# Seven block products of sums in place of eight, in three chunks of each feed-forward of a float32 trunk

## The chip, the cores and the metric

The kernel runs on one core of a Trainium2 chip. The metric is the device time of one launch in microseconds (us), the median of three runs.

## The reference

Four layers, each a half-step feed-forward, an attention (three kinds by turns) and a second half-step feed-forward, on 256 tokens of width 1024, all in float32. The eight feed-forwards are what the change touches:

```python
def rms_norm(x, g, eps=NORM_EPS):
    xf = x.astype(jnp.float32)
    y = xf * lax.rsqrt(jnp.mean(xf * xf, axis=-1, keepdims=True) + eps)
    return (y * g.astype(jnp.float32)).astype(x.dtype)
def swiglu(x, w_in, w_out):
    gate, up = jnp.split(x @ w_in, 2, axis=-1)
    return (jax.nn.silu(gate) * up) @ w_out
```

A half step is h + 0.5 * rms_norm(swiglu(rms_norm(h, g_pre), w_in, w_out), g_post), with w_in 1024 x 5632 and w_out 2816 x 1024.

## The kernel before, in words

The 256 tokens are two tiles t = 0, 1 of 128. For each product the transposed tokens are the weights of TensorE (stationary) and the weight matrix streams past them. Both are split exactly into hi (rounded to float32r) and lo (the rest), and a product is hi x hi + lo x hi + hi x lo: three matmuls for each 128 rows of K. `hilo` (L146) is the split: ScalarE rounds hi (L147), VectorE subtracts to get lo (L148).

`ffn` (L257) cuts the inner width 2816 into five full chunks of 512 (j = 0 to 4) and one of 256 (j = 5). A **unit** (`unit`, L114) is 1 MB of weights, 512 rows by 512 columns of w_in or 256 rows by 1024 of w_out: one DMA on SyncE's queue into a `raw` buffer, then two hi and two lo instructions of 128x1024 each. There are 3 raw buffers, 4 hi/lo pairs for w_in (`wt`) and 3 for w_out (`wo`); a unit waits for its buffer to come free, so the pools decide how far ahead of TensorE the splits run.

In a chunk j from 1 to 4, TensorE runs gate and up for both token tiles (`gate_up`, `product`: four products of 24 matmuls of 512 columns, L144), the four transposes of the result of tile 0 (`turn`, L298), the out product of chunk j-1 for tile 0 (24 matmuls, L236 to L238), the transposes of tile 1 and the out product of tile 1. The transposes are split again into gh (ScalarE) and gl (VectorE, L148). Between these, ScalarE takes silu of the gate (L286) and VectorE multiplies it with up (g, L289).

After the last chunk the feed-forward ends with `finish`: y's mean square, then on VectorE the next sub-layer's input xg (L212, L214), then the update of h (L217, L219), for tile 0 while TensorE still multiplies for tile 1. xg is transposed (tpx, L172) and split into xh and xl, with which the next sub-layer begins.

Each engine works through its own instructions in a fixed order, which is laid down when the program is built; an instruction that waits holds up all that stand behind it on its engine.

## Time and profile before

| | |
|---|---|
| median of 3 runs | 2032.63 us (2032.4 to 2033.66) |
| span of the profiled execution | 2031.3 us |
| TensorE (PE) busy | 2005.6 us, 99% |
| VectorE (DVE) busy | 1260.2 us, 62% |
| ScalarE (ACT) busy | 1033.0 us, 51% |
| TensorE's granted clock | 9 in every slice (90% of full speed or more) |

The span lies 1.33 us below the median. Busy shares are means over the program; within one chunk of a feed-forward they differ, so stretches are read on their own. Matmuls overlap: the time that one adds is the distance from its start to the next one's start, its pitch, not its duration. The same holds for rows of VectorE with a count: first start to last end, of overlapped instructions.

### The profile page before, as it was taken

How to read it: one execution, taken by the hardware profiler on the slowest of the kernel's cores; microseconds unless marked ns; L12 is line 12 of the kernel's file. 1: busy time of each engine (PE TensorE's matmuls, PEld its weight loads, DVE VectorE, ACT ScalarE, POOL GpSimd, SP SyncE). 2: the span in 40 equal slices, each digit the busy share in tenths (PEclk: the TensorE clock that was granted, in tenths of full speed). 3: DMA queues.
4: the chain of work that ended last, by engine and by line, in shares of the span. 5: the costliest groups of instructions: out<-in, count | busy, mean ns of one | idle time of the engine just before them, and what ended most of it. 6: DMA issues, size and time to landing. Idle time of an engine off the chain costs nothing.

```text
span 2031.3 us, 26240 instructions
## 1 busy us (share of the span) xinstructions
PE 2005.6 (99%) x10096; PEld 1659.2 (82%) x10096; DVE 1260.2 (62%) x2051; ACT 1033.0 (51%) x1713; POOL 118.6 (6%) x239
## 2 busy tenths in 40 slices
PE   8999999999999999999999999999999999999998
PEld 6888878888888878888888888678888888878887
DVE  6645678545745666844665568875547545678542
ACT  6443566443543466543454456764445443676441
POOL 0000210000000120000000032000000000210000
PEclk9999999999999999999999999999999999999999
DMA  8654436654656353755376556147554654437550
GB/s 301 224 182 175 163 109 212 224 189 163 210 185 207 125 186 100 254 191 202 125 248 204 203 121 185 44 133 250 197 200 171 209 190 155 157 104 240 205 186 22
DMA packets 168654, 363.19 MB, mean 179 GB/s; under 512 B 7760, under 2 KB 36688, under 8 KB 168528
## 3 DMA queue, kind: packets, MB, share of 16 engines
q1 hardware_dynamic: 168528, 361.51, 52.4%
q8 instruction: 79, 1.29, 0.3%
q14 instruction: 47, 0.39, 0.1%
HBM read 360.43 MB, written 1.05 MB: 178 GB/s over the span
## 4 chain that ended last, share of the span: by engine, by line
PE 94%; DVE 3%; ACT 2%; POOL 1%; issue 0%; DMA 0%; SPq 0%; DVEq 0%; POOLq 0%; ACTq 0%
PE ps L144 47%; PE y L238 9%; PE y L236 9%; PE y L237 9%; PE pw L434 4%; PE pw L435 3%; PE pw L436 3%; PE tpg L298 2%; PE sc L508 1%; DVE lo L148 1%; PE tpx L172 1%; PE tpp L533 1%; PE o L579 1%; PE tpf L465 1%; ACT e L519 0%; ACT hi L147 0%
## 5 line engine op out<-in xcount | busy, mean ns | idle before, releaser
L148 DVE TENSOR_TENSOR lo<-raw,hi 128x1024 fp32r<-128x1024 f32 (+1 forms) x670 | 782.9, 1209 | 481.9 <-ACT hi L147 481.0
L147 ACT CAST hi<-raw 128x1024 fp32r<-128x1024 f32 (+1 forms) x670 | 659.9, 1036 | 412.0 <-PE ps L144 128.6
L144 PE MATMUL ps<-hi,xh 128*128 128x512 f32 (+1 forms) x1536 | 573.6, 373 | 1.2 <-ACT xh L147 1.2
L144 PE MATMUL ps<-hi,xl 128*128 128x512 f32 (+1 forms) x1536 | 572.1, 372 | 0.0
L144 PE MATMUL ps<-lo,xh 128*128 128x512 f32 (+1 forms) x1536 | 571.4, 372 | 0.0
L144 PEld LDWEIGHTS ps<-hi,xh 128*128 128x128 f32 x1536 | 290.0, 189 | 50.8 <-ACT xh L147 1.6
L144 PEld LDWEIGHTS ps<-hi,xl 128*128 128x128 f32 x1536 | 289.8, 189 | 50.9 <-DVE xl L148 0.8
L144 PEld LDWEIGHTS ps<-lo,xh 128*128 128x128 f32 x1536 | 290.1, 189 | 49.9 <-DVE lo L148 0.2
L236 PE MATMUL y<-hi,gh 128*128 128x512 f32 x704 | 281.6, 400 | 0.0
L237 PE MATMUL y<-lo,gh 128*128 128x512 f32 x704 | 274.7, 390 | 0.0
L238 PE MATMUL y<-hi,gl 128*128 128x512 f32 x704 | 274.1, 391 | 0.0
L434 PE MATMUL pw<-hi,xh 128*128 128x512 f32 (+2 forms) x432 | 164.5, 381 | 0.2 <-ACT nat L445 0.2
L286 ACT ACTIVATE sl<-ps,st 128x512 f32<-128x512 f32 (+1 forms) x96 | 62.6, 652 | 196.2 <-issue 149.3
L238 PEld LDWEIGHTS y<-hi,gl 128*128 128x128 f32 x704 | 132.1, 188 | 29.2 <-DVE gl L148 1.3
L435 PE MATMUL pw<-lo,xh 128*128 128x512 f32 (+2 forms) x432 | 155.8, 361 | 0.0
L436 PE MATMUL pw<-hi,xl 128*128 128x512 f32 (+2 forms) x432 | 155.5, 360 | 0.0
L236 PEld LDWEIGHTS y<-hi,gh 128*128 128x128 f32 x704 | 132.3, 188 | 26.0 <-ACT gh L147 1.7
L237 PEld LDWEIGHTS y<-lo,gh 128*128 128x128 f32 x704 | 132.5, 188 | 24.9
L111 POOL TENSOR_TENSOR st<-st,negh 128x1 f32<-128x1 f32 (+1 forms) x56 | 36.8, 658 | 1689.6 <-DVE st L195 1626.3
L147 ACT CAST gh<-tpg 128x512 fp32r<-128x512 f32 (+1 forms) x96 | 51.8, 548 | 150.1 <-PE tpg L298 149.9
L289 DVE SCALAR_TENSOR_TENSOR g<-ps,st,sl 128x512 f32<-128x512 f32 (+1 forms) x96 | 67.5, 704 | 92.9 <-PE ps L144 92.8
L148 DVE TENSOR_TENSOR gl<-tpg,gh 128x512 fp32r<-128x512 f32 (+1 forms) x96 | 61.0, 643 | 62.6 <-ACT gh L147 62.4
(165 smaller groups left out, 1778.2 us busy)
## 6 DMA issues: line engine op xcount, KB each, us to landing
raw<-in_ffn_w_in SPq DMA_DIRECT2D x172, 1024.0 KB, 5.3
raw<-in_ffn_w_out SPq DMA_DIRECT2D x88, 1024.0 KB, 4.9
raw<-in_diff_w_in SPq DMA_DIRECT2D x24, 1024.0 KB, 5.1
raw<-in_moba_w_in SPq DMA_DIRECT2D x12, 1024.0 KB, 5.2
raw<-in_nsa_w_in SPq DMA_DIRECT2D x9, 1024.0 KB, 6.1
raw<-in_diff_w_out SPq DMA_DIRECT2D x8, 1024.0 KB, 4.9
gpre<-in_norm_g SPq DMA_DIRECT2D x12, 512.0 KB, 3.8
gpost<-in_norm_g SPq DMA_DIRECT2D x12, 512.0 KB, 3.8
```

The lines of the kernel that those rows point to most:

```text
L144: nc.tensor.matmul(out, l, r, start=first and i == 0, stop=last and i == len(steps) - 1)
L147: self.nc.scalar.copy(hi, src)
L148: self.nc.vector.tensor_tensor(lo, src, hi.bitcast(F32), op=ALU.subtract)
L236: nc.tensor.matmul(y[b], x[0][:, kt, :], hi[:, k, s], start=f, stop=False)
L237: nc.tensor.matmul(y[b], x[0][:, kt, :], lo[:, k, s], start=False, stop=False)
L238: nc.tensor.matmul(y[b], x[1][:, kt, :], hi[:, k, s], start=False, stop=l)
L286: nc.scalar.activation(sl[t][:, :w], ps[:, :w], AF.Silu, scale=X[t][1])
L289: nc.vector.scalar_tensor_tensor(g[:, :w], ps[:, :w], X[t][1], sl[t][:, :w], op0=ALU.mult, op1=ALU.mult)
L298: nc.tensor.transpose(tp[:, k, :], g[:, k * P:(k + 1) * P], self.ident)
L434: nc.tensor.matmul(out, x[0][:, kt, :], hi[:, k, :], start=first and i == 0, stop=False)
L435: nc.tensor.matmul(out, x[0][:, kt, :], lo[:, k, :], start=False, stop=False)
L436: nc.tensor.matmul(out, x[1][:, kt, :], hi[:, k, :], start=False, stop=last and i == len(todo) - 1)
```

## The change

In chunks 1, 2 and 3 of each feed-forward (`WINO`), gate and up of both token tiles are taken as one 2 x 2 block product (Strassen's in Winograd's form). The tokens are halved by tile and by K (a00 and a01 are tile 0's two halves of K, a10 and a11 tile 1's), the weights by K and by gate/up (b00, b10 gate; b01, b11 up). Seven half-K products of 12 matmuls take the place of eight, of these blocks and sums of them, and their PSUM results are added up.

- `sums` makes the token sums, once for each feed-forward, from the transposed tokens that `xturn` now also copies aside (`keep`): four VectorE instructions of 128x512, and their own hi and lo (sh, sl).
- `plan_wino` makes four weight sums per chunk on VectorE, 128x2048 each: t1 = b00 + b01, t2 = t1 + b11, t3 = b01 + b11, t4 = t2 + b10.
- `wino` runs the seven products into three PSUM banks (pa, pb, pc), copies one to SBUF (p1), and makes gate and up from them with five more VectorE additions of 128x512 (u2, v, g1, g0, sl1) beside the two multiplications that were there.
- Seven units (b00, t2, t3, b10, t1, b11, t4) instead of four are split for each of these chunks, and every split is one hi and one lo instruction of 128x2048 instead of two of 128x1024.
- All weights of a feed-forward, w_out's too, go through one ring: 7 raw buffers (t1 and t2 take two of them) and 4 hi/lo pairs, filled in one list's order (`loads`, `preps`, `fill`). The four PSUM banks of products and transposes are one pool.
- At a feed-forward's end the transposes of chunk 5's tile 1, `turn(last, 1)`, move behind `end(0, ...)` and tile 1's out product of chunk 4.

The built program holds 9758 matmul instructions of TensorE before and 9470 after: 288 fewer, 12 in each of 24 chunks.

```diff
@@ constants and pools @@
+RAWS = 7
+UNITS = 4
+WINO = (1, 2, 3)
...
-        self.wt = pool("wt", 4)
+        self.wt = pool("wt", UNITS)
...
-        self.mm = pool("mm", 2, space=PSUM)
-        self.tp = pool("tp", 2, space=PSUM)
+        self.mm = self.tp = pool("mm", 4, space=PSUM)
...
@@ xturn @@
+        if keep:
+            self.nc.scalar.copy(x.rearrange("p (k n) -> p k n", n=P)[:, 4 * b:4 * b + 4, :], tp)
...
@@ sums @@
+    def sums(self, X, pool, name):
+        v = self.nc.vector
+        half = [[X[t][2][:, b * 512:b * 512 + 512] for b in range(2)] for t in range(NT)]
+        (a00, a01), (a10, a11) = half
+        v.tensor_tensor(a11, a11, a10, op=ALU.subtract)
+        v.tensor_tensor(a10, a00, a10, op=ALU.subtract)
+        v.scalar_tensor_tensor(a00, a11, -1.0, a00, op0=ALU.mult, op1=ALU.subtract)
+        v.scalar_tensor_tensor(a01, a01, -1.0, a00, op0=ALU.mult, op1=ALU.subtract)
+        out = []
+        for t in range(NT):
+            sh = pool.tile([P, KD, P], F32R, tag="sh", name=f"sh{name}_{t}")
+            sl = pool.tile([P, KD, P], F32R, tag="sl_", name=f"sl_{name}_{t}")
+            src = X[t][2].rearrange("p (k n) -> p k n", n=P)
+            self.hilo(src, sh, sl)
+            out.append((sh, sl))
+        return out
...
@@ ffn @@
-                self.tc.tile_pool(name=f"wo{l}{f}", bufs=3, reuse_waits="tile") as wo:
...
+            def split(n, of, done=False):
+                live["unit"] += 1
+                self.n += 1
+                nk, w, m = shape.get(of, (4, 512, 4))
+                hi = self.wt.tile([P, nk, w], F32R, tag="hi", name=f"hi{self.n}")
+                lo = self.wt.tile([P, nk, w], F32R, tag="lo", name=f"lo{self.n}")
+                v = R[of][:, :nk * w].rearrange("p (k n) -> p k n", n=w)
+                for k in range(0, nk, m):
+                    self.hilo(v[:, k:k + m], hi[:, k:k + m], lo[:, k:k + m])
+                if done:
+                    free(of)
+                U[n] = hi, lo, nk, w
...
+                for n, src in (("b00", quarter(0, 0)), ("b01", quarter(0, 1)), ("t1", None), ("t2", None),
+                               ("b11", quarter(1, 1)), ("b10", quarter(1, 0))):
+                    loads.append(lambda n=n, src=src: raw(name(n), src))
...
+                def t12():
+                    add("t1", "b00", "b01")
+                    add("t2", "t1", "b11")
+                    split(name("t2"), name("t2"))
+                def t3():
+                    add("b01", "b01", "b11")
+                    split(name("t3"), name("b01"), True)
+                def t4():
+                    add("t2", "t2", "b10")
+                    free(name("b10"))
+                    split(name("t4"), name("t2"), True)
...
+                preps.append((name("b00"), lambda: split(name("b00"), name("b00")), 4))
+                preps.append((name("t2"), lambda: (t12(), free(name("b00"))), 6))
+                preps.append((ko[0], lambda: split(ko[0], ko[0], True), 5))
+                preps.append((name("t3"), t3, 0))
+                preps.append((name("b10"), lambda: split(name("b10"), name("b10")), 2))
+                preps.append((name("t1"), lambda: split(name("t1"), name("t1"), True), 0))
+                preps.append((ko[1], lambda: split(ko[1], ko[1], True), 1))
+                preps.append((name("b11"), lambda: split(name("b11"), name("b11"), True), 0))
+                preps.append((name("t4"), t4, 0))
+            def fill():
+                while loads and live["raw"] < RAWS:
+                    loads.pop(0)()
+                while preps and live["unit"] < UNITS:
+                    preps.pop(0)[1]()
+                    while loads and live["raw"] < RAWS:
+                        loads.pop(0)()
...
+            def wino(j, nr):
+                def times(ps, x, at, n, first, stop, shut=True):
+                    self.product(ps, x, [(at, unit((j, n)))], first, stop, more=True)
+                    close((j, n))
+                def o(t, k):
+                    out(j - 1, t, (k,))
+                    if t == 1:
+                        close((j - 1, "o", k))
+                    fill()
+                two = lambda name: pool.tile([P, 512], F32, tag=name, name=f"{name}{l}{f}_{j}", bufs=1)
+                add = lambda d, x, z: nc.vector.tensor_tensor(d, x, z, op=ALU.add)
+                (s24, s31), A, B, C = SUMS, bank("pa"), None, None
+                p1, u2, v = two("p1"), two("u2"), two("v")
+                times(A, X[0][0], 0, "b00", True, True)
+                nc.scalar.copy(p1, A)
+                fill()
+                turn(j - 1, 0)
+                B = bank("pb")
+                times(B, s24, 0, "t2", True, True)
+                add(u2, B, p1)
+                fill()
+                o(0, 0)
+                C = bank("pc")
+                times(C, s31, 0, "t3", True, True)
+                fill()
+                turn(j - 1, 1)
+                times(A, X[0][0], 4, "b10", False, True)
+                sl0 = gate(0, A, 512, j)
+                fill()
+                o(1, 0)
+                times(B, s31, 4, "t1", False, True)
+                add(v, B, p1)
+                g1 = pool.tile([P, 512], F32, tag="g", name=f"g{l}{f}_{j}_1")
+                add(g1, C, v)
+                fill()
+                o(0, 2)
+                times(B, s24, 4, "b11", False, True)
+                g0 = pool.tile([P, 512], F32, tag="g", name=f"g{l}{f}_{j}_0")
+                add(g0, B, p1)
+                up(0, g0, 512, sl0, j, nr[0], g0)
+                fill()
+                times(C, X[1][0], 4, "t4", False, True)
+                sl1 = pool.tile([P, 512], F32, tag="sl", name=f"sl{l}{f}_{j}_1")
+                add(sl1, C, u2)
+                nc.scalar.activation(sl1, sl1, AF.Silu, scale=X[1][1])
+                up(1, g1, 512, sl1, j, nr[1], g1)
...
-            gate_up(last)
-            u = out_units(last - 1)
-            out(last - 1, 0, u)
-            turn(last, 0)
-            turn(last, 1)
-            ahead()
-            u2 = out_units(last)
-            out(last, 0, u2)
-            turn_x = end(0, y[0])
-            out(last - 1, 1, u)
-            turn_x()
-            out(last, 1, u2)
-            self.later_x = end(1, y[1])
+            plain(last, zig, [lambda: turn(last - 1, 0), lambda: turn(last - 1, 1)])
+            out(last - 1, 0, (0, 2))
+            turn(last, 0)
+            ahead()
+            out(last, 0, (0,))
+            turn_x = end(0, y[0])
+            out(last - 1, 1, (0, 2))
+            for k in (0, 2):
+                close((last - 1, "o", k))
+            turn(last, 1)
+            turn_x()
+            out(last, 1, (0,))
+            self.later_x = end(1, y[1])
```

What VectorE's order becomes between the second and the third of the full chunks 1 to 3, shown in layer 1's first feed-forward. Before, from the end of chunk 2's splits to chunk 3's g (g_j_t and gl_j_t carry chunk and tile):

```order
L148 TENSOR_TENSOR lo_4906<-raw_4903,hi_4905 128x1024
L148 TENSOR_TENSOR gl_2_0_4803<-tpg_2_0_4797,gh_2_0_4802 128x512
L148 TENSOR_TENSOR lo_4906<-raw_4903,hi_4905 128x1024
L148 TENSOR_TENSOR lo_5031<-raw_5028,hi_5030 128x1024 x2
L148 TENSOR_TENSOR gl_2_1_4852<-tpg_2_1_4846,gh_2_1_4851 128x512
L148 TENSOR_TENSOR lo_5039<-raw_5036,hi_5038 128x1024 x2
L148 TENSOR_TENSOR lo_5104<-raw_5101,hi_5103 128x1024 x2
L148 TENSOR_TENSOR lo_5112<-raw_5109,hi_5111 128x1024 x2
L289 SCALAR_TENSOR_TENSOR g_3_0_4990<-ps_3_10_4965,st_4161,sl_3_0_4936 128x512
L148 TENSOR_TENSOR lo_5120<-raw_5117,hi_5119 128x1024 x2
L289 SCALAR_TENSOR_TENSOR g_3_1_5017<-ps_3_11_4992,st_4247,sl_3_1_4963 128x512
```

After, the same stretch:

```order
L364 TENSOR_TENSOR raw_4724<-raw_4655,raw_4674 128x2048
L473 TENSOR_TENSOR g_2_0_4848<-pb_4706,p_2_4677 128x512
L364 TENSOR_TENSOR raw_4754<-raw_4724,raw_4801 128x2048
L419 SCALAR_TENSOR_TENSOR g_2_0_4848<-g_2_0_4848,st_4444,sl_2_0_4776 128x512
L473 TENSOR_TENSOR sl_2_1_4871<-pc_4737,u_2_4678 128x512
L364 TENSOR_TENSOR raw_4674<-raw_4674,raw_4801 128x2048
L152 TENSOR_TENSOR lo_4854<-raw_4754,hi_4853 128x2048
L419 SCALAR_TENSOR_TENSOR g_2_1_4818<-g_2_1_4818,st_4446,sl_2_1_4871 128x512
L152 TENSOR_TENSOR lo_4876<-raw_4782,hi_4875 128x2048
L152 TENSOR_TENSOR lo_4895<-raw_4674,hi_4894 128x2048
L152 TENSOR_TENSOR lo_4918<-raw_4803,hi_4917 128x2048
L152 TENSOR_TENSOR gl_2_0_4927<-tpg_2_0_4921,gh_2_0_4926 128x512
```

Between a chunk's g and the next one's stand the additions of 128x2048 (L364: t1, t2, t3 of chunk 3), and the splits of t2, of a w_out unit, t3 and b10, all behind one another; the multiplications and additions for g stand between them.

VectorE at the end of layer 0's second feed-forward (gl_5_t is the split of chunk 5's transposes). Before:

```order
L148 TENSOR_TENSOR gl_5_0_4088<-tpg_5_0_4084,gh_5_0_4087 128x256
L148 TENSOR_TENSOR gl_5_1_4095<-tpg_5_1_4091,gh_5_1_4094 128x256
L193 TENSOR_SCALAR st_4130<-st_4128 128x1
L212 TENSOR_TENSOR yx_4139<-y_0_0_3193,gpre_4098 128x512
L195 SCALAR_TENSOR_TENSOR st_4135<-st_4133,st_4130 128x1
L212 TENSOR_TENSOR yx_4139<-y_0_1_3194,gpre_4098 128x512
L214 SCALAR_TENSOR_TENSOR xg_4100<-yx_4139,st_4137,xg_4100 128x512 x2
L217 TENSOR_TENSOR yg_4146<-y_0_0_3193,gpost_2925 128x512
L217 TENSOR_TENSOR yg_4146<-y_0_1_3194,gpost_2925 128x512
L219 SCALAR_TENSOR_TENSOR h_85<-yg_4146,st_4137,h_85 128x512 x2
```

After:

```order
L201 SCALAR_TENSOR_TENSOR st_4118<-st_4116,st_4113 128x1
L218 TENSOR_TENSOR yx_4122<-y_0_1_3103,gpre_4089 128x512
L220 SCALAR_TENSOR_TENSOR xg_4091<-yx_4122,st_4120,xg_4091 128x512 x2
L223 TENSOR_TENSOR yg_4129<-y_0_0_3102,gpost_2927 128x512
L223 TENSOR_TENSOR yg_4129<-y_0_1_3103,gpost_2927 128x512
L225 SCALAR_TENSOR_TENSOR h_82<-yg_4129,st_4120,h_82 128x512 x2
L152 TENSOR_TENSOR lo_4265<-raw_4248,hi_4264 128x2048
L199 TENSOR_SCALAR st_4137<-st_4135 128x1
L152 TENSOR_TENSOR gl_5_1_4174<-tpg_5_1_4170,gh_5_1_4173 128x256
L152 TENSOR_TENSOR xl_4124<-tpx_4177,xh_4123 128x512
```

gl_5_1, which stood right behind gl_5_0 and ahead of `finish`, now stands behind tile 0's yx, xg, yg and h and behind a lo of 128x2048 of the next sub-layer.

## Rows read from the trace of the kernel before

**Rows 1.** Page: busy time by engine; share of the last chain by engine.
```profile
PE 2005.6 (99%) x10096; PEld 1659.2 (82%) x10096; DVE 1260.2 (62%) x2051; ACT 1033.0 (51%) x1713; POOL 118.6 (6%) x239
...
PE 94%; DVE 3%; ACT 2%; POOL 1%; issue 0%; DMA 0%; SPq 0%; DVEq 0%; POOLq 0%; ACTq 0%
```
**Rows 2.** Chain of waits, in one full chunk: start, us, what.
```profile
1059.96 15.42 PE ps L144 x68
1075.38 0.44 PE tpg L298 x4
```
**Rows 3.** Windows, one chunk: PE, PEld, DVE, ACT, POOL; clock, DMA share, GB/s.
```profile
1062.90:1096.50 33.60, 33.60 (x154) 27.78 (x153) 16.68 (x16) 14.09 (x18) 0.00 (x0) 1.00 0.56 188
```
**Rows 4.** Timeline of VectorE, the same chunk: start, us, what, [idle before].
```profile
1015.39 4.63 DVE L148 TENSOR_TENSOR lo<-raw,hi 128x1024 fp32r<-128x1024 f32 x4 [0.99 <-ACT hi L147]
...
1062.94 2.36 DVE L148 TENSOR_TENSOR lo<-raw,hi 128x1024 fp32r<-128x1024 f32 x2 [8.58 <-ACT hi L147]
...
1076.10 0.75 DVE L289 SCALAR_TENSOR_TENSOR g<-ps,st,sl 128x512 f32<-128x512 f32 x1
1076.76 1.22 DVE L148 TENSOR_TENSOR lo<-raw,hi 128x1024 fp32r<-128x1024 f32 x1
1077.89 0.68 DVE L148 TENSOR_TENSOR gl<-tpg,gh 128x512 fp32r<-128x512 f32 x1
1078.49 3.49 DVE L148 TENSOR_TENSOR lo<-raw,hi 128x1024 fp32r<-128x1024 f32 x3
...
1096.57 2.36 DVE L148 TENSOR_TENSOR lo<-raw,hi 128x1024 fp32r<-128x1024 f32 x2 [8.57 <-ACT hi L147]
```
**Rows 5.** VectorE by line and shape: busy us, mean ns, idle before.
```profile
L148 DVE TENSOR_TENSOR lo<-raw,hi 128x1024 fp32r<-128x1024 f32 x650 | 769.6, 1225 | 477.9 <-ACT hi L147 477.0
...
L1046 DVE TENSOR_TENSOR gpre<-gpre,gpost 128x1024 f32<-128x1024 f32 x11 | 13.7, 1248 | 1.6 <-DMA gpost<-in_norm_g 1.4
...
L148 DVE TENSOR_TENSOR lo<-raw,hi 128x512 fp32r<-128x512 f32 x16 | 10.1, 681 | 3.8 <-ACT hi L147 3.8
```
**Rows 6.** ScalarE by line and shape.
```profile
L147 ACT CAST hi<-raw 128x1024 fp32r<-128x1024 f32 x650 | 648.3, 1048 | 409.8 <-PE ps L144 128.6 <-issue 96.2 <-PE y L238 66.9
...
L147 ACT CAST hi<-raw 128x512 fp32r<-128x512 f32 x16 | 9.0, 618 | 2.2 <-DMA raw<-in_ffn_w_in 2.1
```
**Rows 7.** Timelines of VectorE, ScalarE and TensorE at a feed-forward's end.
```profile
190.03 0.76 DVE L148 TENSOR_TENSOR gl<-tpg,gh 128x256 fp32r<-128x256 f32 x2 [2.61 <-ACT gh L147]
...
194.68 1.42 DVE L214 SCALAR_TENSOR_TENSOR xg<-yx,st,xg 128x512 f32<-128x512 f32 x2
...
197.34 1.41 DVE L219 SCALAR_TENSOR_TENSOR h<-yg,st,h 128x512 f32<-128x512 f32 x2
...
193.15 0.60 ACT L190 ACTIVATE junk<-y 128x512 f32<-128x512 f32 x1 [0.73 <-PE y L238]
...
197.88 1.03 PE L172 MATMUL tpx<-ident,xg 128*128 128x128 f32 x8
```
**Rows 8.** Windows, the program's start; columns as in rows 3.
```profile
11.00:15.30 4.30, 4.16 (x9) 2.98 (x10) 4.30 (x8) 4.27 (x10) 0.55 (x1) 1.00 1.05 385
```
**Rows 9.** DMA issues: line, queue, count, KB each, median us to landing.
```profile
raw<-in_ffn_w_in SPq DMA_DIRECT2D x172, 1024.0 KB, 5.3
```
**Rows 10.** Timeline of TensorE after two of its waits.
```profile
11.14 0.79 PE L144 MATMUL ps<-hi,xh 128*128 128x512 f32 x1 [1.18 <-ACT xh L147]
...
15.31 0.47 PE L144 MATMUL ps<-hi,xh 128*128 128x512 f32 x1
...
1229.56 0.65 PE L465 MATMUL tpf<-ident,nat 128*128 128x128 f32 x4 [1.38 <-POOL nat L458]
...
1230.29 0.28 PE L436 MATMUL pw<-hi,xl 128*128 128x256 f32 x1
1230.41 0.28 PE L434 MATMUL pw<-hi,xh 128*128 128x256 f32 x1
```

More of the change, by code (lines that the diff above doesn't have):

```diff
@@ L131, in split_unit, with product @@
         return hi, lo, nk, w
-    def product(self, out, x, units, first=True, last=True, cols=None):
+    def product(self, out, x, units, first=True, last=True, cols=None, more=False):
         nc = self.nc
@@ L143, in product @@
         for i, (l, r) in enumerate(steps):
-            nc.tensor.matmul(out, l, r, start=first and i == 0, stop=last and i == len(steps) - 1)
+            nc.tensor.matmul(out, l, r, start=first and i == 0, stop=last and i == len(steps) - 1,
+                             skip_group_check=more)
     def hilo(self, src, hi, lo):
@@ L197, in mean_square, with finish @@
         return v
-    def finish(self, t, y, gpost, half, x=None, gg=None):
+    def finish(self, t, y, gpost, half, x=None, gg=None, keep=False):
         nc = self.nc
@@ L221, in finish @@
             rest = self.rms(t)
[L222 removed]
+            return (X, rest, x), lambda: [self.xturn(x, b, X, keep) for b in range(2)]
         return None, lambda: None
@@ L328, in ffn, with plain @@
-            ahead()
-            u2 = out_units(last)
-            out(last, 0, u2)
-            turn_x = end(0, y[0])
-            out(last - 1, 1, u)
+                n = chunks[j][1] // P
+                self.out_product(t, y[t], G[j, t], [(k, unit((j, "o", k))) for k in ks],
+                                 j == 0 and 0 in ks, j == last and n - 2 in ks)
+            def plain(j, order, between=()):
+                w = chunks[j][1]
+                hs = (0, 1) if w == 512 else (0,)
+                between = list(between)
+                sl = {}
+                for i, (which, t) in enumerate(order):
+                    ns = [(j, "gu"[which], h) for h in hs]
+                    ps = bank("ps")
+                    self.product(ps[:, :w], X[t][0], [(4 * h, unit(n)) for h, n in zip(hs, ns)])
+                    self.turn_x()
+                    if which == 0:
+                        sl[t] = gate(t, ps, w, j)
+                    else:
+                        up(t, ps, w, sl[t], j, X[t][1])
+                    if (which, 1 - t) in order[:i]:
+                        for n in ns:
+                            close(n)
+                    fill()
+                    if between:
+                        between.pop(0)()
@@ new lines, in ffn @@
+            plan_plain(0)
+            for j in range(1, last):
+                if j in WINO:
+                    plan_wino(j)
+                else:
+                    plan_plain(j)
+                    plan_out(j - 1)
+            plan_plain(last)
+            plan_out(last - 1)
+            plan_out(last)
+            plain(0, [(0, 0), (1, 0), (0, 1), (1, 1)])
+            if WINO:
+                SUMS = self.sums(X, pool, f"{l}{f}")
+                nr = []
+                for t in range(NT):
+                    r = self.stat()
+                    nc.vector.tensor_scalar(r, X[t][1], -1.0, None, op0=ALU.mult)
+                    nr.append(r)
@@ L1048, in end @@
             def end(t, y):
-                after[t], turn_x = self.finish(t, y, gpost, kind == "ffn", xs[t], gg)
+                keep = not last and phases[i + 1][1] == "ffn"
+                after[t], turn_x = self.finish(t, y, gpost, kind == "ffn", xs[t], gg, keep)
                 if last:
```

152 lines of the change are left out of this document (100 added, 52 removed).

## Prediction, made before the changed kernel was run

> **What bounds the kernel now.** First the page: TensorE is busy 99% of the span, VectorE 62%, ScalarE 51%, and the chain that ends last is TensorE's for 94% [rows 1]. Next, what TensorE does inside a chunk: in the chain of waits 68 matmuls of 512 columns take 15.42 us, so each adds 0.2268 us, and a group of four transposes adds 0.44 us [rows 2]. A full chunk has 96 matmuls for gate and up, 48 for the out product and two groups of transposes: 144 x 0.2268 + 0.88 = 33.54 us. The same place in the next chunk comes 1096.57 - 1062.94 = 33.63 us later [rows 4]. So TensorE does nothing but multiply there, at granted clock 1.00, the 2.4 GHz level [rows 3].
>
> The page's 62% for VectorE is a mean. In a chunk it works 16.68 us of 33.60, ScalarE 14.09 [rows 3]. This half-empty VectorE is what the change spends, and the window, not the page, is where it is priced.
>
> **What TensorE saves.** 288 matmuls x 0.2268 = 65.3 us, if every one was on the end-setting path and nothing else becomes late. A changed chunk is 132 x 0.2268 + 0.88 = 30.8 us of TensorE.
>
> In rows 2 the pitch is 226.8 ns. The Trainium skill ("TensorE: Matmul & The Clock Gate", section "Back-to-back issue gap") gives about 131 ns for sustained matmuls of 512 columns; by that the saving would be an estimated 37.7 us and the time 27.6 us above what each case below says. The trace does not agree, and its number is used.
>
> **What VectorE is given.** Its operation of 128x2048 has no row. The 128x1024 subtraction lasts 1.225 us, the 128x512 one 0.681 [rows 5], so a further element costs 544/512 = 1.0625 ns. Back to back, four of 1024 end after 4.63 us [rows 4], so one adds (4.63 - 1.225)/3 = 1.135 us. Then 2048 adds 1.135 + 1.088 = 2.22 us. Bounds: twice 1.135 is 2.27, if nothing is saved by joining two; 2.18, if the 1.2 us instruction's fixed part shrinks as the multiplication of 1024 (1.248) and the subtraction (1.225) differ [rows 5], by some 0.04. The additions of 2048 float32 are taken at the same 2.22, since the 1024 multiplication lies within 2% of the subtraction. Small operations of 128x512: 0.60 for two tensors (1078.49 - 1077.89), 0.66 for three operands (1076.76 - 1076.10) [rows 4].
>
> The skill ("VectorE: DVE Perf Modes", section "The perf-mode tier table") says that float32 tensor_tensor has no faster mode, with about 2.29 us for 2048 elements. No row here has that shape; by 2.29 alone the 35 operations below would cost 2.4 us more in each of eight feed-forwards.
>
> A changed chunk has nine splits and four weight sums, 13 x 2.22 = 28.9 us, two gl and five additions of results, 7 x 0.60 = 4.2, and two multiplications, 1.3: 34.4 us. That is more than TensorE's new 30.8 and more than the 33.63 that the chunk took before. **VectorE becomes the bound in three of five full chunks.** ScalarE does not: nine hi of some 1.9 us (1.048 + 1024 x 0.84 ns, from 1.048 and 0.618 [rows 6]), p1, two silu and two gh stay near 21 us. Nor does the DMA: nine raw loads become seven (the sums need none), a 1 MB load lands in 5.3 us [rows 9], and at the start the queue carried 385 GB/s [rows 8] against 188 in a chunk [rows 3].
>
> **The changed chunks, step by step.** The ring has four hi/lo pairs, so VectorE can't store up work: at the start of chunk 1 only three sums and two splits (b00, t2) of that chunk are done. I follow VectorE's new order from TensorE's start of chunk 1 to the addition for g1 in chunk 3, for which TensorE must wait before it may add t4's product to the same bank.
> - 0.8 us: the last g of chunk 0.
> - 35 operations of 2048: 77.7 us.
> - Two sl of 1024 for the token sums: 2.3 us.
> - 21 small two-tensor operations and 6 of three operands: 12.6 + 4.0 = 16.6 us.
> - 1.8 us in which VectorE itself waits: t1's hi can't be made until a product frees a pair, and t1's lo follows it.
>
> Together 99.2 us. Behind it stand t4's 12 matmuls and 9 of the out product, 21 x 0.2268 = 4.8: the stretch ends at 104.0, where three chunks took 3 x 33.63 = 100.9. So +3.1 us for a feed-forward, in place of -8.5 by TensorE alone; TensorE waits 11.6 us in the three chunks. The longest waits fall in chunk 1 before the product with the token sums (some 3.1 us, sh) and before b10's lo (2.2), and in chunk 3 before t2's lo (2.1).
>
> Five feed-forwards have just this list: 15.5. Layer 0's second has four more xg operations in the stretch, of which the 1.8 us idle takes part: +4.2. The last, with two tiny ones more: +3.2. The first has 34 large, no token sums, 19 and 4 small: 0.8 + 75.5 + 11.4 + 2.6 + 2.3 idle + 4.8 = 97.4, or -3.5. **Sum +19.4 us.** Chunks 0, 4 and 5 keep their pace: VectorE has six large and four small operations there, some 16 us in 33.6, and TensorE's 48 out matmuls (10.9 us) cover two splits of the next chunk (2 x (1.9 + 2.22) = 8.2).
>
> **The end of each feed-forward.** Before, both gl of chunk 5 were done at 190.8, ahead of `finish` [rows 7]. Now gl_5_1 stands behind it. Count from E = 193.1, when tile 0's y is complete and ScalarE takes its square (193.15). xg is done at 196.10 and h at 198.75, E + 5.65 [rows 7]. Then the next sub-layer's lo of 2048, 2.22, a tiny operation, and gl itself: E + 8.4. Meanwhile TensorE has 21 matmuls of tile 1's out product (4.8), two transposes for gl_5_1 (0.2), the tpx that stood at 197.88 [rows 7] (0.8) and two matmuls with hi before it needs gl: E + 6.25. TensorE waits 2.2 us, with all of tile 1's `finish` and the next sub-layer's first product queued behind it on the same engine. Seven times 2.2 and some 0.7 in the last feed-forward, where no lo of a next one stands between: **+16.1 us.** The lower bound is 0, if the lo happens to come after gl in time (its hi is late); the upper is one more lo, 2.2 more each, 34 in all.
>
> **Sum.** 2031.3 + 19.4 + 16.1 = 2066.8 for the span; the median lies 1.3 us above the span: **2068 us.**
>
> **Rivals.**
> *Slower still: each wait costs more than itself.* After the long idle at the program's start TensorE's matmuls came at (15.31 - 11.14)/9 = 0.46 us each [rows 10], twice the pitch, though the granted clock of that stretch reads 1.00 [rows 8]: some 2 us lost. If the new waits of 2 to 3 us do the same, 2 to 4 times in each feed-forward, it is 8 x 2 x 2 = 32 to 64 us more: 2100 to 2132. Against it: after a wait of 1.38 us the matmuls of 256 columns came at once at 0.12 us [rows 10], full pace. What decides is which of the two rows a wait of 2 to 3 us is like. 13%.
> The skill's same TensorE page (section "Part 1: The HAM clock gate") has a clock that falls when the engine idles and must be earned back; that is this rival's rule, and of the rows the first pair would agree, the second not.
> *Faster: TensorE keeps the pace.* For it: VectorE is idle half of a chunk now. The condition is VectorE's work of a changed chunk below 30.8 us, which needs the large operation at 1.94 us or less (30.8 - 5.5 = 25.3 over 13). Then the 65.3 come through: 1967, or 1984 with the end's 16.1. Against it: nothing in the rows has an element below 1.06 ns. 10%.
> *Between: the loss is smaller.* If the end's wait is hidden it is 2052. If besides that the splits run further ahead than the ring's order suggests (chunk 4's splits stand among chunk 3's small operations in VectorE's order, three of them, 6.7 us, of which one is in my list), 2030 to 2045; with a large operation of 2.13 us in addition each stretch breaks even and it is 2032 or a little less. 22%, of which 6 below 2030.
> That the change does not do what it says is excluded: the built program has the 288 matmuls less.
>
> **How the numbers follow.** The forecast, VectorE as the bound in the changed chunks and a wait at each end, has 55%, with 2045 to 2085 as its own range: the large operation between 2.18 and 2.27 gives -11 to +14 (8 x 35 x 0.04 or 0.05), and the end's wait goes from nothing (2052) to one more lo (2083). Range for 8 in 10: from 2015, which leaves out the 10% of the faster rival and some 3% of the case between, to 2110, which leaves out the larger half of the slower rival (7%). Of no change within 0.2%, some 4 us and about what a measurement of this kernel can tell, that is 2028.6 to 2036.7, only the case between holds a part: 6%. Faster: 10% + 6% = 16%. Slower: 78%.
>
> **What would show it.** Right: in a window over chunks 1 to 3 VectorE is busy above 95% and TensorE near 89%, with some 104 us for the three; TensorE's idle time stands against lo and sl of L152 and additions of L364 on VectorE, not against ScalarE or DMA; the 128x2048 groups of VectorE have a mean of 2.2 to 2.35 us; and at a feed-forward's end an idle of about 2 us stands before the first y matmul that takes gl_5_1. Wrong: large operations near 1.9 us; VectorE with idle time in the changed chunks; matmuls at 0.4 us apart behind each wait; waits in chunks 0, 4 or 5; or idle time there that ends on a DMA.

## The result, and the profile after

The changed kernel takes 2135.77 us (median, 2132.09 to 2137.81), the kernel before 2032.52 beside it: a ratio of 1.0504, 95% interval 1.0489 to 1.0519. It is slower by some 103 us. The forecast was slower, 2068 us, with a range up to 2110: the sign held, and the size was a third of the real one.

The page of the changed kernel, engines and last chain; beside [rows 1]:

```profile
PE 2013.6 (94%) x9808; PEld 1623.3 (76%) x9808; DVE 1713.7 (80%) x2143; ACT 1188.4 (56%) x1597; POOL 135.0 (6%) x239
...
PE 71%; DVE 17%; issue 5%; ACT 5%; DMA 2%; POOL 1%; SPq 0%; DVEq 0%; POOLq 0%; ACTq 0%
```

TensorE has 288 matmuls less and is busy 8 us longer; VectorE has 17% of the last chain where it had 3%. Where the time lies is read from windows. Layer 1's first feed-forward, chunks 1 to 4, columns as in [rows 3], TensorE's timeline giving the cuts (the first matmul of each chunk):

```profile
1072.86:1115.20 42.34, 35.76 (x142) 27.70 (x141) 37.90 (x27) 20.05 (x15) 0.00 (x0) 0.92 0.49 172
1115.20:1146.79 31.59, 31.59 (x142) 25.54 (x141) 31.13 (x23) 17.64 (x14) 0.00 (x0) 1.00 0.56 190
1146.79:1181.17 34.38, 32.41 (x142) 25.47 (x141) 33.84 (x24) 22.77 (x16) 0.00 (x0) 1.00 0.72 251
1181.17:1215.08 33.91, 33.91 (x154) 27.85 (x153) 20.03 (x16) 14.30 (x11) 0.00 (x0) 1.00 0.46 159
```

Chunk 4 is a plain (unchanged) one. Of the three changed ones VectorE is busy 99% in chunk 2 and 98% in chunk 3, which ends after 34.4 us, VectorE's own list; chunk 1 takes 42.3, where VectorE is idle too and the granted clock falls to 0.92. VectorE's large operations cost what was reckoned (mean 2286 and 2281 ns; back to back 2.20):

```profile
L152 DVE TENSOR_TENSOR lo<-raw,hi 128x2048 fp32r<-128x2048 f32 x332 | 754.1, 2286 | 186.1 <-ACT hi L151 184.8
L364 DVE TENSOR_TENSOR raw<-raw,raw 128x2048 f32<-128x2048 f32 x96 | 218.4, 2281 | 3.0 <-DMA raw<-in_ffn_w_in 3.0
```

The same cuts in all eight feed-forwards of both traces, in us. A pair of transpose groups in each feed-forward has moved from chunks 0 to 3 into chunk 5 (7.0 us in all); the column "like for like" has that put right. The fifth row includes the attention layers; the first 11 us of the program, ahead of TensorE's first product, stand in no row.

| stretch | before | after | more | like for like | forecast |
|---|---|---|---|---|---|
| chunk 0, first feed-forward | 26.1 | 43.0 | 16.9 | 17.3 | 0 |
| chunk 0, the seven others | 161.4 | 172.7 | 11.3 | 14.4 | 0 |
| chunks 1 to 3 | 811.3 | 857.1 | 45.8 | 49.3 | 19.4 |
| chunks 4 and 5 | 362.0 | 371.3 | 9.3 | 2.3 | 0 |
| end of one to the start of the next, and the tail | 659.4 | 678.7 | 19.2 | 19.2 | 16.1 |
| span | 2031.3 | 2133.7 | 102.4 | 102.4 | 35.5 |

So 67 us are to be explained: some 32 in chunks 0, which the prediction took as unchanged, and 30 in chunks 1 to 3.

### The profile page after: what moved, and what is told of

Read it like the earlier page. It is cut to its first block, busy times and chain, and to the rows that moved or that the text cites. A ratio compares the mean times of both kernels' runs of the same rounds, so it can differ in the third digit from the quotient of the medians.

```text
span 2133.7 us, 25622 instructions
## 1 busy us (share of the span) xinstructions
PE 2013.6 (94%) x9808; PEld 1623.3 (76%) x9808; DVE 1713.7 (80%) x2143; ACT 1188.4 (56%) x1597; POOL 135.0 (6%) x239
## 4 chain that ended last, share of the span: by engine, by line
PE 71%; DVE 17%; issue 5%; ACT 5%; DMA 2%; POOL 1%; SPq 0%; DVEq 0%; POOLq 0%; ACTq 0%
PE ps L147 18%; DVE lo L152 8%; PE y L244 7%; PE y L242 7%; PE y L243 7%; PE pb L147 6%; PE pc L147 5%; PE pa L147 4%; PE pw L655 4%; PE pw L656 3%; PE pw L657 3%; DVE raw L364 3%; ACT hi L151 2%; DMA raw<-in_ffn_w_in 2%; PE tpg L427 1%
## 5 line engine op out<-in xcount | busy, mean ns | idle before, releaser
L152 DVE TENSOR_TENSOR lo<-raw,hi 128x2048 fp32r<-128x2048 f32 (+2 forms) x482 | 926.1, 1940 | 235.5 <-ACT hi L151 233.8
L151 ACT CAST hi<-raw 128x2048 fp32r<-128x2048 f32 (+2 forms) x482 | 774.8, 1624 | 552.1 <-PE ps L147 110.5
L147 PE MATMUL ps<-hi,xh 128*128 128x512 f32 (+1 forms) x768 | 278.2, 363 | 4.2 <-ACT xh L151 2.4
L147 PE MATMUL ps<-lo,xh 128*128 128x512 f32 (+1 forms) x768 | 275.0, 358 | 3.9 <-DVE st L199 2.2
L147 PE MATMUL ps<-hi,xl 128*128 128x512 f32 (+1 forms) x768 | 273.7, 358 | 0.3
L364 DVE TENSOR_TENSOR raw<-raw,raw 128x2048 f32<-128x2048 f32 x96 | 218.4, 2281 | 3.0 <-DMA raw<-in_ffn_w_in 3.0
L147 PEld LDWEIGHTS ps<-hi,xh 128*128 128x128 f32 x768 | 146.6, 191 | 27.2 <-ACT xh L151 4.5
L147 PEld LDWEIGHTS ps<-lo,xh 128*128 128x128 f32 x768 | 146.6, 191 | 27.0 <-DVE lo L152 6.9
L147 PEld LDWEIGHTS ps<-hi,xl 128*128 128x128 f32 x768 | 146.4, 191 | 22.4 <-DVE st L199 1.1
L147 PE MATMUL pb<-hi,sh 128*128 128x512 f32 x288 | 117.9, 409 | 14.7 <-ACT sh L151 14.7
```

The costliest lines, as they stand in the source:

```text
L147: nc.tensor.matmul(out, l, r, start=first and i == 0, stop=last and i == len(steps) - 1, skip_group_check=more)
L151: self.nc.scalar.copy(hi, src)
L152: self.nc.vector.tensor_tensor(lo, src, hi.bitcast(F32), op=ALU.subtract)
L364: nc.vector.tensor_tensor(R[name(to)], R[name(a)], R[name(b)], op=ALU.add)
```

## The experiments

**First set: undo one part each.** The first keeps the ring and the order and takes the seven products back; the second leaves the four weight sums of each changed chunk out (two of their buffers get a load of their own instead); the third moves the second token tile's load; the fourth moves the last transposes back.

```diff
-WINO = (1, 2, 3)
+WINO = ()
```

> All of the change but the seven products: no chunk is a block product (WINO is empty), so the ring, the 128x2048 splits, the merged PSUM pool and the moved transposes stay, and all 96 gate and up matmuls are back. Theory 1 (the changed chunks cost what VectorE's list in them costs; beside that the ring delays the first feed-forward's second token tile, and the ends wait): chunks 1 to 3 of a feed-forward come back to about 101.4 us, chunk 0 of the later feed-forwards to 23.1, the first chunk 0 stays near 43, the ends stay 2.3 us longer; 2032.5 + 17 + 10 + 17 = 2077 us, 2068 to 2088. Rival (the ring itself, four pairs for everything and splits of double length, makes TensorE wait in all chunks): chunks 1 to 3 stay above 105 and the time above 2110.

2096.36 us, ratio 1.0312 (1.0296 to 1.0327), above the 2068 to 2088 expected. Chunks 1 to 3 are back at 101.6 us, 33.9 each; in the kernel before a chunk takes 33.6, so the ring makes a plain chunk some 0.3 us longer. That and two more terms were undersized. The first chunk 0 ends 21.4 us later than in the kernel before (17 expected), since TensorE waits 19.2 us in it for the second tile's tokens, behind eleven loads of 1 MB; in the changed kernel it is 14.65 us behind nine. The ends keep their cost (+20.5 us for 17 expected), and so do the other chunks 0 (+11.2 us, or +14.2 like for like): these costs come from the ring and the order, not from the products.

```diff
-                for n, src in (("b00", quarter(0, 0)), ("b01", quarter(0, 1)), ("t1", None), ("t2", None),
+                for n, src in (("b00", quarter(0, 0)), ("b01", quarter(0, 1)), ("t1", quarter(0, 0)), ("t2", quarter(0, 0)),
...
-                    add("t1", "b00", "b01")
-                    add("t2", "t1", "b11")
...
-                    add("b01", "b01", "b11")
...
-                    add("t2", "t2", "b10")
```

> The four weight sums of 128x2048 per changed chunk are left out (the result is not that of the reference); in their place two buffers get a load of their own, so every split and product stays. Theory 1 (VectorE's list is the bound): a changed chunk's list falls by 4 x 2.20 = 8.8 us to 25.6, below TensorE's 30.8, so chunks 2 and 3 come at 31 and chunk 1 at 33 to 37; chunks 1 to 3 from 108.3 to 95 to 99, eight times some 11 less: 2136 - 90 = 2046, 2030 to 2070. Rival (the waits come from the ring's four pairs and from TensorE at half pace behind each wait, not from VectorE's load): chunks 1 to 3 keep 104 to 108 and the time stays above 2100.

2041.40 us, within the 2030 to 2070. The three changed chunks of the same feed-forward, columns as in [rows 3]:

```profile
1032.44:1063.86 31.42, 31.42 (x142) 25.55 (x140) 30.41 (x25) 19.66 (x15) 0.00 (x0) 1.00 0.83 292
1063.86:1095.52 31.66, 31.66 (x141) 25.42 (x140) 25.90 (x19) 19.86 (x15) 0.00 (x0) 1.00 0.79 266
1095.52:1127.16 31.64, 31.64 (x142) 25.48 (x140) 25.90 (x19) 19.87 (x15) 0.00 (x0) 1.00 0.80 267
```

With VectorE's list at 25.9 us instead of 34.4, TensorE never stops in them and the clock stays at 1.00: 8.8 us less work on VectorE in each chunk took 13.6 us off three chunks in this feed-forward (108.3 to 94.7). The ring's four pairs are the same, and so are the 1 MB loads, now two more in each chunk. That settles that VectorE is the bound of the changed chunks. Chunk 1 comes at TensorE's pace too, although the token sums are still made in it.

```diff
-        self.later_x = lambda: start(1)
+        start(1)
+        self.later_x = lambda: None
```

> Only the program's start is changed: tile 1's tokens are loaded, normed and transposed before the first weights and not behind the ring's seven loads. Theory 1 (the first feed-forward's 16.9 us are this load's place on SyncE's queue): chunk 0 of the first feed-forward from 42.9 to 27 to 30 us, the time 13 to 16 us less, 2120 to 2123. Rival (the first chunk waits for weights or for the sums on VectorE): it stays above 36 us, and the time within 7 us of 2136.

2126.18 us, 9.6 less, where 13 to 16 were expected. Chunk 0 of the first feed-forward did fall from 43.0 to 27.9 us. In the changed kernel the second tile's tokens are asked for behind nine loads of the ring, of which the first four go in quarters (its timelines of SyncE's queue, ScalarE and TensorE):

```profile
2.27 12.08 SPq L310 DMA_DIRECT2D raw<-in_ffn_w_in  x18
14.70 0.37 SPq L310 DMA_DIRECT2D raw<-in_ffn_w_out  x1
15.52 2.76 SPq L310 DMA_DIRECT2D raw<-in_ffn_w_in  x2
18.33 1.21 SPq L1238 DMA_DIRECT2D h<-in_x  x1
...
32.77 0.63 ACT L196 ACTIVATE junk<-h 128x512 f32<-128x512 f32 x1 [9.86 <-DMA h<-in_x]
...
33.95 1.97 PE L176 MATMUL tpx<-ident,xg 128*128 128x128 f32 x8 [14.65 <-DVE xg L168]
```

Issued at 18.33, used at 32.77, and TensorE waits 14.65 us; in the kernel before four loads stood ahead of them. Of the 15.1 us won, 5.3 are lost again in chunks 1 to 3 of that feed-forward (99.1 to 104.4); a likely reason, not tried by itself, is that VectorE had got ahead while TensorE stood still.

```diff
             turn(last, 0)
+            turn(last, 1)
             ahead()
...
-            turn(last, 1)
             turn_x()
```

> Only the last transposes are moved back: those of chunk 5's tile 1 stand ahead of the end of tile 0 again. Theory 1 (their lo stands behind the finish on VectorE, and TensorE waits 2.2 us at each end): the stretch from a feed-forward's last gate and up matmul to the next one's first falls from 20.0 to 17.7 us, seven times, 14 to 17 us in all: 2119 to 2122. Rival (the wait is taken over by tile 0's transposed input or by the next weights): 20.0 stays 19 or more, and the time within 7 us of 2136.

2122.36 us, 13.4 less (14 to 17 expected). The stretch from a feed-forward's last gate and up matmul to the first of the feed-forward right behind it falls from 20.0 to 18.0 us. What ends the wait in the changed kernel, at the end of layer 0's second feed-forward (timelines of TensorE, ScalarE and VectorE):

```profile
1046.27 0.50 PE L242 MATMUL y<-hi,gh 128*128 128x512 f32 x1 [1.78 <-ACT gh L151]
...
1043.44 1.90 ACT L151 CAST hi<-raw 128x2048 fp32r<-128x2048 f32 x1 [0.88 <-PE y L244]
...
1045.87 0.35 ACT L151 CAST gh<-tpg 128x256 fp32r<-128x256 f32 x1
...
1046.45 0.41 DVE L152 TENSOR_TENSOR gl<-tpg,gh 128x256 fp32r<-128x256 f32 x1
```

It is ScalarE's gh, which stands behind a hi of 128x2048 of the next feed-forward just as gl stands behind the lo: here the prediction's step was right in size, and named the second of two queues. But only three of the seven ends have a feed-forward right behind them. Ahead of an attention layer the same wait is half as long, as ahead of layer 1's:

```profile
1243.82 0.50 PE L242 MATMUL y<-hi,gh 128*128 128x512 f32 x1 [0.93 <-ACT gh L151]
```

All eight waits of this kind in the changed kernel, the last of 0.46 us included, make 9.5 us. In the profiled executions the ends take 7.5 us less with the transposes moved back (678.7 to 671.2), so 11.7 of their 19.2 us stay.

**Second set: where the changed chunks stand, and who does the sums.** The first of these also has the edits of the third and fourth runs above.

```diff
-                    nc.vector.tensor_tensor(R[name(to)], R[name(a)], R[name(b)], op=ALU.add)
+                    nc.gpsimd.tensor_tensor(R[name(to)], R[name(a)], R[name(b)], op=ALU.add)
```

> Everything is computed; the four weight sums of each changed chunk run on GpSimd in place of VectorE, tile 1's tokens come first at the program's start, and the last transposes stand ahead of the end of tile 0. Theory 1 (VectorE's list is the bound, and the first load and the last transposes are costs of their own): the chunks as without the sums, 94.7 us for three; from that run's 2041 the first load takes some 25 (its chunk 0 ended at 65.9, with tile 1 first some 39), the transposes 13: 2003, with GpSimd's sums in time, and 1995 to 2030 if they are late in places. Rival (GpSimd, slower by element, and VectorE get in each other's way, or the sums are late): the three chunks stay above 103 and the time above 2070.

2354.80 us, ratio 1.1582 (1.1564 to 1.1599): the rival's way; chunks 1 to 3 take 134 to 141 us in each feed-forward. GpSimd and VectorE by line and shape, and two rows of the timeline:

```profile
L364 POOL TENSOR_TENSOR raw<-raw,raw 128x2048 f32<-128x2048 f32 x96 | 501.3, 5231 | 471.7 <-DVE lo L152 398.4 <-DMA raw<-in_ffn_w_in 58.1 <-DVE st L199 12.8
...
L152 DVE TENSOR_TENSOR lo<-raw,hi 128x2048 fp32r<-128x2048 f32 x332 | 959.4, 2900 | 232.3 <-ACT hi L151 232.3
...
1192.40 6.58 POOL L364 TENSOR_TENSOR raw<-raw,raw 128x2048 f32<-128x2048 f32 x1 [4.50 <-DVE lo L152]
...
1195.11 6.02 DVE L152 TENSOR_TENSOR lo<-raw,hi 128x2048 fp32r<-128x2048 f32 x1
```

A sum takes GpSimd 5.23 us in the mean, and VectorE's subtraction beside it 6.02 in place of 2.29 (2.90 in the mean of all 332), so the work has not left VectorE. The Trainium skill ("GPSIMD Engine Reference", section "1. Specifications") says that GpSimd shares its SBUF interfaces with VectorE, with contention where VectorE reads two inputs from SBUF; these rows agree.

```diff
-WINO = (1, 2, 3)
+WINO = (2, 3, 4)
```

> The three changed chunks are 2, 3 and 4 in place of 1, 2 and 3, so that a plain chunk stands between the start of a feed-forward, where the token sums are made, and the first changed chunk. Theory 1 (chunk 1's 42.3 us are the bound's list with the token sums, their waits and TensorE's half pace behind these): the first changed chunk falls by some 4 to 5 us to 37 or 38, the others stay 31.6 and 34.4, the time 30 to 40 us less, 2096 to 2106. Rival (the first changed chunk is long because the ring has to be refilled at the passage from plain to changed chunks, whatever the sums): it stays above 41, the time above 2125.

2074.71 us, 61 less than with chunks 1 to 3 and more than the 30 to 40 expected. Chunks 1 to 4, columns as in [rows 3]:

```profile
1049.76:1083.62 33.86, 33.86 (x154) 27.84 (x152) 30.37 (x22) 13.78 (x11) 0.00 (x0) 1.00 0.44 148
1083.62:1115.15 31.53, 31.53 (x141) 25.45 (x140) 27.52 (x18) 18.00 (x13) 0.00 (x0) 1.00 0.60 200
1115.15:1148.38 33.23, 31.91 (x141) 25.48 (x140) 32.82 (x24) 17.56 (x14) 0.00 (x0) 1.00 0.54 181
1148.38:1182.76 34.38, 32.40 (x142) 25.48 (x141) 32.76 (x23) 22.81 (x16) 0.00 (x0) 1.00 0.64 223
```

This is the plainest picture of the bound. In the plain chunk, where the token sums now stand, VectorE works 30.4 of 33.9 us and gets ahead; the first changed chunk behind it runs at TensorE's pace, 31.5; the second has used up the lead, 33.2; the third comes at VectorE's list, 34.4.

```diff
-WINO = (1, 2, 3)
+WINO = (2,)
```

> One changed chunk, the second, in each feed-forward. Theory 1 (VectorE's 34.4 us of list in a changed chunk can be spread over the plain ones around it as far as the ring reaches, five or six large operations): chunk 2 comes near TensorE's 30.8, at 31 to 33, the plain ones stay 33.7; against the run with the ring alone (2096) 1 to 3 us less in each feed-forward: 2072 to 2088. Rival (a changed chunk costs its list wherever it stands): chunk 2 takes 35 or more and the time is 2105 or above.

2075.91 us, within the 2072 to 2088. Chunk 2 takes 31.55 us, with VectorE 25.3 of them, the plain ones 33.9. One changed chunk alone is worth 2.3 us, and two more behind it nothing (2074.71).

The last of this set gives TensorE work where it waited, in chunk 1 of each feed-forward:

```diff
+DUMMY = 16
...
                 B = bank("pb")
+                if j == 1:
+                    xr = X[0][0][0].rearrange("p k n -> p (k n)")
+                    for _ in range(DUMMY):
+                        nc.tensor.matmul(B, X[0][0][0][:, 0, :], xr[:, :512], start=True, stop=True, skip_group_check=True)
```

> The changed kernel with 16 matmuls of 512 columns more in chunk 1 of each feed-forward, on data that is there and into a bank that is started anew behind them, so they change no result: they fill 3.6 us of the 3.4 us that TensorE waits at two places before b10's lo. Theory A (behind a wait TensorE runs at 0.43 us a matmul for a while, and that lengthens chunk 1): the matmuls behind the filled wait come 0.23 us apart, chunk 1 gets 1 to 2 us shorter in spite of the added work, 2120 to 2130. Theory B (VectorE's list alone sets chunk 1's length): the pace is full, but chunk 1 stays within 0.5 us and the time within 5 us of 2136. Rival (the pace has nothing to do with waits): the 0.43 us stay.

2122.91 us: 12.9 less, with 128 matmuls more. First the changed kernel's TensorE in chunk 1 (start, duration, what, idle before), then both kernels' windows in that place:

```profile
1078.22 0.50 PE L147 MATMUL pa<-hi,xh 128*128 128x512 f32 x1 [2.04 <-ACT hi L151]
...
1081.30 0.79 PE L147 MATMUL pa<-lo,xh 128*128 128x512 f32 x1 [1.40 <-DVE lo L152]
...
1082.32 0.63 PE L147 MATMUL pa<-hi,xh 128*128 128x512 f32 x1
1082.75 0.63 PE L147 MATMUL pa<-lo,xh 128*128 128x512 f32 x1
...
1090.34 0.50 PE L147 MATMUL pb<-hi,sh 128*128 128x512 f32 x1 [2.93 <-ACT sh L151]
```
```profile
1076.00:1081.00 5.00, 1.87 (x7) 0.86 (x5) 5.00 (x4) 2.65 (x3) 0.00 (x0) 1.00 0.70 234
1081.00:1086.00 5.00, 4.70 (x14) 3.76 (x15) 4.85 (x6) 0.00 (x0) 0.00 (x0) 0.66 0.50 185
1090.34:1095.34 5.00, 4.78 (x15) 3.63 (x16) 4.92 (x5) 2.08 (x3) 0.00 (x0) 0.66 0.02 3
```

And with the waits filled (its places are 4 us earlier; the last window is layer 0's second feed-forward, behind the same wait of 2.93 us for sh):

```profile
1072.02 3.90 PE L485 MATMUL pb<-xh 128*128 128x512 f32 x16
...
1077.49 0.39 PE L148 MATMUL pa<-hi,xl 128*128 128x512 f32 x1
1077.72 0.40 PE L148 MATMUL pa<-hi,xh 128*128 128x512 f32 x1
...
1084.76 0.50 PE L148 MATMUL pb<-hi,sh 128*128 128x512 f32 x1 [2.93 <-ACT sh L152]
```
```profile
1076.00:1081.00 5.00, 4.94 (x22) 3.70 (x21) 5.00 (x5) 0.00 (x0) 0.00 (x0) 1.00 0.70 254
1084.76:1089.76 5.00, 4.38 (x19) 3.14 (x20) 5.00 (x5) 2.07 (x3) 0.00 (x0) 1.00 0.20 78
888.07:893.07 5.00, 4.77 (x15) 3.62 (x16) 4.92 (x5) 2.06 (x3) 0.00 (x0) 0.66 0.18 68
```

In the changed kernel the matmuls behind the waits come 0.43 us apart, at a granted clock of 0.66 in these windows (a mean of the lower level, 1.2 GHz, and the full one). Behind the filled place they come 0.23 apart at 1.00. The later wait of 2.93 us is still there to the hundredth. Here the pace behind it is full too, but that is the exception: five feed-forwards have this wait, and in the other four the clock falls behind it as in the changed kernel (0.66 or 0.67 over 5 us). So the run takes away the half pace behind the first two waits, and not behind the third. Chunks 1 to 3 of the seven later feed-forwards together fall from 758.0 to 744.9 us. So theory A holds for the place that was filled, at 1.9 us for each of them; of the 11 us by which chunk 1 exceeds TensorE's pace it explains these two, and not the rest, in which the half pace behind the third wait still stands.

**Third set: the token sums, and a version that gains.**

```diff
-                SUMS = self.sums(X, pool, f"{l}{f}")
+                SUMS = [X[t][0] for t in range(NT)]
```

> The changed kernel, chunks 1 to 3, without the token sums: their products take the tokens of tile 0 and 1 themselves, so the result is not the reference's; every product, split and weight sum stays. Theory 1 (chunk 1 is long by the token sums, 4.9 us of VectorE's list, and by TensorE's wait for them): chunk 1 from 42.3 to 35 to 37, the others as they were, the time 40 to 60 us less, 2076 to 2096. Rival (the ring's refill at the passage into the first changed chunk is what costs): chunk 1 stays above 40, the time above 2115.

2067.10 us, 69 less, more than the 40 to 60 expected. Chunks 1 to 3, columns as in [rows 3]:

```profile
1044.55:1075.86 31.31, 31.31 (x142) 25.51 (x141) 31.04 (x20) 17.73 (x13) 0.00 (x0) 1.00 0.64 233
1075.86:1108.97 33.11, 31.78 (x142) 25.46 (x140) 32.85 (x23) 17.46 (x14) 0.00 (x0) 1.00 0.52 178
1108.97:1143.31 34.34, 32.17 (x141) 25.43 (x140) 33.98 (x25) 22.96 (x16) 0.00 (x0) 1.00 0.72 254
```

Here the token sums and their hi and lo are left out, and the products take the tokens themselves. Chunk 1 falls from 42.3 to 31.3, although VectorE's list lost only some 4.9 us; the ring's refill at the passage is as it was. The steps 31, 33, 34.4 are those of the run with chunks 2 to 4. So the whole excess of chunk 1 goes with the token sums. It goes with the weight sums as well (31.4 us in the second run of the first set): chunk 1 is long only where both stand in VectorE's list. Why 11 us and not 5 is seen in the changed kernel's chunk 1, VectorE and then ScalarE:

```profile
1078.37 0.68 DVE L269 TENSOR_TENSOR xg<-xg 128x512 f32<-128x512 f32 x1
1078.97 2.28 DVE L152 TENSOR_TENSOR lo<-raw,hi 128x2048 fp32r<-128x2048 f32 x1
1081.17 0.68 DVE L270 TENSOR_TENSOR xg<-xg,xg 128x512 f32<-128x512 f32 x1
...
1085.17 0.68 DVE L272 SCALAR_TENSOR_TENSOR xg<-xg 128x512 f32<-128x512 f32 x1
1089.38 2.29 DVE L152 TENSOR_TENSOR lo<-raw,hi 128x2048 fp32r<-128x2048 f32 x1 [3.52 <-ACT hi L151]
...
1087.45 1.90 ACT L151 CAST hi<-raw 128x2048 fp32r<-128x2048 f32 x1 [8.79 <-PE pa L147]
1089.25 1.99 ACT L151 CAST sh<-xg 128x1024 fp32r<-128x1024 f32 x2
```

The token sums are ready at 1085.85 (L272). But sh stands on ScalarE behind t1's hi, which waits for a pair that only b10's product frees; that product (pa) had waited for b10's lo (1078.97, done 1081.2), held up by the first token sum ahead of it, and then ran at half pace. A ring: VectorE's list makes TensorE late, TensorE's late product holds a buffer, the buffer holds ScalarE's queue, and sh in that queue holds TensorE and VectorE again (3.52 us idle on VectorE).

Two last runs put together what had paid: changed chunks 2 and 4 only, each with a plain chunk ahead; tile 1's tokens first; the last transposes moved back. The second of them also splits the units in halves again.

```diff
-WINO = (1, 2, 3)
+WINO = (2, 4)
```

> Two changed chunks, 2 and 4, with a plain one ahead of each; tile 1's tokens first at the program's start; the last transposes ahead of the end of tile 0. Theory 1 (a changed chunk comes at TensorE's pace where a plain chunk ahead of it lets VectorE get ahead; the other costs are separate): against the run with chunk 2 alone (2076) a second chunk at 31.6 in place of 33.9 in eight feed-forwards (18), the transposes (14) and the first load (24) less: 2020, 2012 to 2030, below the kernel before. Rival (VectorE is short again by the fourth chunk, or the end takes the gain back): above 2033.

2028.51 us, ratio 0.9974 (0.9964 to 0.9984) to the kernel before; 2020 was expected, 2012 to 2030 as the range.

```diff
                 nk, w, m = shape.get(of, (4, 512, 4))
+                m = min(m, nk // 2)
```

> The same with every split as two instructions of 128x1024 on ScalarE and VectorE in place of one of 128x2048, as in the kernel before. Theory 1 (chunk 0's extra 1 to 4 us come from long splits that stand ahead of tile 1's input on VectorE and ScalarE, and from TensorE waiting for a whole unit): chunk 0 from 24.4 towards 23.3 in the later feed-forwards, 5 to 10 us less in all than the run in whole splits; the changed chunks stay at 31.6 although VectorE's list grows by 9 x 0.07 us. Rival (the order, not the length, holds tile 1's input up): within 3 us of the run in whole splits.

2021.68 us, ratio 0.9942 (0.9930 to 0.9953): faster than both kernels, 11 to 12 us below the one before. Its chunks 1 to 4:

```profile
1012.28:1046.14 33.86, 33.86 (x153) 27.85 (x152) 31.08 (x29) 14.43 (x17) 0.00 (x0) 1.00 0.41 141
1046.14:1077.71 31.57, 31.57 (x142) 25.46 (x140) 25.54 (x26) 20.62 (x23) 0.00 (x0) 1.00 0.82 268
1077.71:1111.60 33.89, 33.89 (x153) 27.85 (x152) 26.54 (x23) 14.25 (x17) 0.00 (x0) 1.00 0.36 122
1111.60:1143.16 31.56, 31.56 (x141) 25.46 (x140) 25.54 (x26) 20.62 (x23) 0.00 (x0) 1.00 0.60 202
```

Plain and changed chunks by turns: VectorE works 31.1, 25.5, 26.5 and 25.5 us, never the bound, and TensorE never stops. The halves gave 6.8 us over the run in whole splits, 4.5 of them in chunks 0 (168.5 to 164.0 for the seven later ones). That a shorter split stands ahead of tile 1's input and that TensorE can begin on half a unit would both do this; which of them it was, the run does not tell.

## Why the prediction was wrong

- *The bound.* Right. VectorE's list of 34.4 us for a changed chunk is what chunk 3 takes (34.4), the large operations cost 2.20 where 2.22 was reckoned, and without the weight sums the chunks run at TensorE's pace. The rival in which TensorE keeps the pace fell. (The lower bound of 2.18 takes off "some 0.04" where the two rows differ by 0.02; nothing hangs on it.)
- *Chunks 1 to 3: +19.4 forecast, +49.3 measured.* The term was mis-sized in one step, "1.8 us in which VectorE itself waits". In chunk 1 VectorE waits 3.52 and 0.80 us and some tenths, 4.4 of the 42.34 in all, and over the three chunks 5.4 (108.31 less 102.88 busy): the product that frees the pair for t1's hi came late and at half pace, and sh stood behind that hi. The reckoning has no slower pace in it. The stretch ended 108.3 us after its start instead of 104.0, and after 106.8 to 109.2 in the other feed-forwards with token sums in chunk 1. The rest of the sum holds: without the token sums it would give 104.0 - 4.9 = 99.1, and that run took 98.8. TensorE's waits were foreseen in place and nearly in size: 3.1 us before sh (2.93 measured), 2.2 before b10's lo (2.04 for its hi and 1.40 for its lo), 2.1 before t2's lo in chunk 3 (1.45).
- *Half pace behind a wait* was a rival at 13%, priced at 32 to 64 us on top, 2100 to 2132 in all. The measured time lies next to that, but only part of the gap is this rival's: it does happen, not behind every wait, and filling one place gave 12.9 us in all. What was left of it behind the wait for sh was not tried. (The clock of 1.00 that the prediction reads in [rows 8] beside the slow start says nothing: that trace has no record of the clock before 15.5 us.) The forecast's own signs of being wrong, matmuls 0.4 us apart behind waits and waits in chunks 0, both came.
- *Chunk 0 of the first feed-forward: 0 forecast, +17.3 measured.* Missed. The prediction did not follow what the ring's seven raw buffers do to SyncE's queue: nine loads stand ahead of tile 1's tokens, where four stood. TensorE waits 14.65 us for them and works at a granted clock of 0.50, the 1.2 GHz level, for some 6 us behind that wait. The sentence "Nor does the DMA" looked at the rate [rows 8, 9], where the place in the queue decided. (Its "nine raw loads become seven" is wrong besides: a full chunk has four loads of w_in and two of w_out in both kernels.) It even took 3.5 us off the first feed-forward for its early token sums; that gain is there (99.1 us for the three chunks against 101.5), bought with the long chunk 0: it is gone where tile 1 comes first (104.4).
- *Chunks 0 of the others: 0 forecast, +14.4 measured.* "Chunks 0, 4 and 5 keep their pace" fell for chunk 0. In the changed kernel TensorE waits 6.9 us in these seven, for hi and xh of ScalarE and lo and small statistics (st) of VectorE, where it did not wait before; in one of them the granted clock falls to a mean of 0.94. Splits of double length stand ahead of the second tile's input; with halves, in the last two runs, the chunks were 4.5 us shorter. What makes up the rest was not taken apart.
- *The ends: +16.1 forecast, +19.2 measured.* Right in place, and near in size in part by luck. The wait for the last transposes is there at each end (ScalarE's gh comes last, not gl), but it measures 1.78 us at three ends and 0.93 or less at the others, 9.5 us in all for 16.1. Moving the transposes back shortens the ends by 7.5 us in the profiled executions (the whole kernel by 13.4 in the medians). The other 11.7 us lie mostly in the stretches with an attention layer (the longest, 181.0 us before, takes 185.8), which the forecast did not count; their cause stays open.
- *The range* ended at 2110, in the lower part of the half-pace rival, and beside that rival every term was counted for the three changed chunks and the ends alone. The stretches on which nothing was changed on purpose were taken as unchanged.

## What to carry to other kernels

Before trading work of the bound engine for work of another, add up the other engine's list for that stretch, not for the program: here 62% busy had room for one changed chunk in two, and not for three in a row. A shared ring of buffers is also an order of queues: ask for each wait on a free buffer what stands behind it on that engine, and for each early load what it goes ahead of. Small operations that something waits for at once (here sums of the tokens, and the hi that follows) want a place ahead of the long ones, which was not tried, or work between them and their use, as the plain chunk gives it in the last runs.
